# Two of four weight sums in a Strassen-Winograd product moved from VectorE to accumulating DMA

## The chip, the cores and the metric

The kernel runs on one core of one Trainium2 chip. A core has TensorE (matmuls), VectorE (DVE in the profile), ScalarE (ACT), GpSimd (POOL) and SyncE (SP), which work side by side and meet at semaphores, and 16 DMA engines that move data between DRAM and SBUF. The metric is the time of one launch on the device, in microseconds (us); lower is better.

## The reference

One block of a transformer-like network on 512 tokens with 2048 features, all in float32. What matters here is its last part, the feed-forward network:

```python
def conv_ffn(h, w_up, conv_w, conv_b, w_down):
    u, g = jnp.split(h @ w_up, 2, -1)
    return (u * jax.nn.silu(dwconv3(g, conv_w, conv_b))) @ w_down
...
        hx = modulate(x, sh2, sc2)
        fx = from_rows(conv_ffn(to_rows(hx), w_up[l], ffn_conv_w[l], ffn_conv_b[l], w_down[l]))
        x = layer_norm(ALPHA * x + g2 * fx, ln2_g[l], ln2_b[l])
```

`w_up` is 2048 x 11264 (two halves of 5632 columns, `u` and `g`) and `w_down` is 5632 x 2048. The depthwise convolution runs over rows of 64 tokens. Ahead of it stand a modulation from `w_ada`, an input projection, a gated recurrence in two directions, pooling and convolution mixers, and an output projection.

## The kernel before

The kernel runs through stages in this order: input projection and modulation (`ramp`), the recurrence and the other mixers (`heads`, `local`), the output projection (`out_half`), the up product (`up_half` for the first two pairs of column blocks, `up_pair` for the other 20) and the down product (`down`, `finish`). A scheduler sets the order of each engine's instructions from the order of the code and from priorities; loads and splits of weights stand under `high_priority(offset=AHEAD)`, so they come in the queues some 600 instructions earlier than the code has them. Tiles come from pools with a number of buffers per tag; a load waits until the buffer's last reader is done.

Matmuls reach float32 precision by splitting each operand into a high part H (a cast to `float32r` on ScalarE) and a low part L (the difference, on VectorE), with three matmuls for a product (`mm3`, lines 109 to 111: high by high, low by high, high by low).

The up product of a pair of column blocks (256 columns) is done by Winograd's form of Strassen's scheme: the 2048 x 256 weights are cut into halves by rows and by columns, the tokens into two halves of 256, and seven products of half size take the place of eight. The scheme needs four sums of the activations (`S1` to `S4`, made once in `combine`), four sums of the weights (made for each block in `weights7`), and sums of the products (`Z`, at the end of `up_block`). A tile `W` has, for each of its row blocks of 128, seven slots of 128 columns: four raw quarters and the four sums, one of which is built in place of a raw quarter. In numbers: slots 0 and 1 are the lower rows' left and right columns, slot 2 is the upper left, and slot 3 holds the upper right until the first sum is written over it.

`up_pair` runs `up_block` for the `g` half of the columns, the gate (`gate_conv`, the sigmoid and a product), `up_block` for the `u` half, and the last product with its store to DRAM (`h_d`). `up_block` has eight row blocks. Before, `weights7` loads and sums four of them at once (`NB`), in a tile with two buffers: two loads of 512 KB on SyncE's queue, three VectorE operations (lines 971 to 973, of which the first makes two sums), and then, for each two row blocks (`NU`, a unit), `parts`: one cast on ScalarE (line 954) and one difference on VectorE (line 955), into tiles H and L with three buffers each. TensorE runs the 42 matmuls of a unit product by product, in the order `for pr in (1, 2, 3, 7, 5, 6, 4)`. There are 20 pairs, 2 blocks each, 4 units a block: 160 units.

`down` takes the weights of the down product in loads of up to six row blocks of 512 columns, in the same `W` tag, and splits three at a time. `finish` does the last three row blocks together with the closing layer norm.

Of the kernel before, what the change touches and what calls it, by code (L numbers as in the profile page):

```python
# [40 lines left out]
NB, NU = 4, 2  # L41
# [31 lines left out]
class Kernel:  # L73
# [810 lines left out]
    def combine(self, cp, raw, k2s):  # L884
# [37 lines left out]
    def up_half(self, cp, p, hf):  # L922
# [15 lines left out]
        for i in range(2):  # L938
# [3 lines left out]
            s = cp.tile([P, n], F32, name=f"cs_{f}_{hf}", tag="cs", bufs=2)  # L942
# [15 lines left out]
    def weights7(self, ww, name, src, c0):  # L958

        nc = self.nc
        tt = nc.vector.tensor_tensor
        with self.tc.high_priority(offset=AHEAD):
            W = ww.tile([P, NB, 7, P], F32, name=f"W_{name}", tag="W", bufs=2)
            for r0, s0 in ((c0, 2), (c0 + KT // 2, 0)):
                nc.sync.dma_start(out=vw(W[:, 0, 0, :], [[7 * P, NB], [1, 2 * P]], s0 * P),
                                  in_=src[r0 * P:(r0 + NB) * P].rearrange("(k p) c -> p k c", p=P))
            pair = lambda a, b: vw(W[:, 0, 0, :], [[7 * P, NB], [(b - a) * P, 2], [1, P]], a * P)  # L970
            tt(out=pair(4, 3), in0=pair(3, 1), in1=pair(2, 3), op=ALU.subtract)  # L971
            tt(out=W[:, :, 5], in0=W[:, :, 1], in1=W[:, :, 4], op=ALU.subtract)
            tt(out=W[:, :, 6], in0=W[:, :, 0], in1=W[:, :, 5], op=ALU.subtract)  # L973
            units = []
            for c in range(0, NB, NU):
                units += self.parts(ww, f"{name}_{c}", W[:, c:c + NU].rearrange("p a s m -> p (a s m)"), 7 * NU * P),
        return units

    def up_block(self, ww, ep, name, src):
# [19 lines left out]
        tt = nc.vector.tensor_tensor
        Z = ep.tile([P, 6, 256], F32, name=f"Z_{name}", tag="Z", bufs=2)  # L1000
# [6 lines left out]
        tt(out=two(2, 3), in0=vw(X[2][:, :], [[0, 2], [1, 256]]), in1=two(4, 5), op=ALU.add)  # L1007
# [58 lines left out]
    def weights_down(self, ww, name, pieces):  # L1066

        nc = self.nc
        with self.tc.high_priority(offset=AHEAD):
            n = sum(m for _, m in pieces)  # L1070
            W = ww.tile([P, 7, 512], F32, name=f"W_{name}", tag="W", bufs=2)
            o = 0
            for src, m in pieces:
                nc.sync.dma_start(out=W[:, o:o + m], in_=src.rearrange("(k p) c -> p k c", p=P))
                o += m
            out = []
            for a in range(0, n, 3):
                m = min(3, n - a)
                H, Lw = self.parts(ww, f"{name}_{a}", W[:, a:a + m].rearrange("p k c -> p (k c)"), 512 * m)
                out += [(H[:, 512 * i:512 * i + 512], Lw[:, 512 * i:512 * i + 512]) for i in range(m)]  # L1080
        return out

    def down(self, ww, dn, f0, n, first):
        w = self.I["w_down"][0]
# [4 lines left out]
        for j in range(4):  # L1089
            banks = self.banks4(f"dn_{f0}_{j}")  # L1090
            for q0 in range(0, n, 6):
                m = min(6, n - q0)
                r0 = (f0 + q0) * P
                wt = self.weights_down(ww, f"dn_{f0}_{j}_{q0}", [(w[r0:r0 + m * P, 512 * j:512 * j + 512], m)])
# [9 lines left out]
    def finish(self, ww, cp, f0, n):  # L1104
        nc, I, w = self.nc, self.I, self.I["w_down"][0]
        for f in range(f0, f0 + n):
            self.load_h(cp, f)
        cols = lambda j: (w[f0 * P:(f0 + n) * P, 512 * j:512 * j + 512], n)
        wt = self.weights_down(ww, "rs_0", [cols(0), cols(1)])
        with self.tc.high_priority(offset=AHEAD):  # L1110
            W = ww.tile([P, 7, 512], F32, name="W_rs_1", tag="W", bufs=2)
            R = ww.tile([P, 7, 512], F32R, name="R_rs_1", tag="W", bufs=2)
            for i, j in enumerate((3, 2)):
                nc.sync.dma_start(out=W[:, i * n:(i + 1) * n], in_=cols(j)[0].rearrange("(k p) c -> p k c", p=P))
# [119 lines left out]
```

## Time and profile before

| | |
|---|---|
| median of three runs | 2746.2 us (2740.33 to 2747.18) |
| the profiled execution: time, span | 2748.07 us, 2746.3 us |
| mean granted TensorE clock | 0.981 |
| moved by DMA | 416.14 MB, mean 152 GB/s |
| GpSimd instructions in the stage from 1425 to 2245 us | none |

A row of the stage view gives the busy time of each engine in one stretch of the span. A row of the wait view reads: engine and line that waited, what it waited for, total us, number of times, the longest. A row of the group view gives line, engine, operation, output and inputs with their shapes, count, busy us and mean ns, then the idle time of the engine just before. A row of the tile view gives the shortest, median and longest duration in ns and the first and the last start. A row on DMA issues ends with the size of one transfer and the median time from issue to landing. A row of the timeline gives start, duration, engine, line and, in brackets, the idle time before it and what ended it.

### The profile page before, as it was taken

How to read it: one execution, taken by the hardware profiler on the slowest of the kernel's cores; microseconds unless marked ns; L12 is line 12 of the kernel's file. 1: busy time of each engine (PE TensorE's matmuls, PEld its weight loads, DVE VectorE, ACT ScalarE, POOL GpSimd, SP SyncE). 2: the span in 40 equal slices, each digit the busy share in tenths (PEclk: the TensorE clock that was granted, in tenths of full speed). 3: DMA queues.
4: the chain of work that ended last, by engine and by line, in shares of the span. 5: the costliest groups of instructions: out<-in, count | busy, mean ns of one | idle time of the engine just before them, and what ended most of it. 6: DMA issues, size and time to landing. Idle time of an engine off the chain costs nothing.

```text
span 2746.3 us, 39980 instructions
## 1 busy us (share of the span) xinstructions
PE 2579.1 (94%) x16332; PEld 2257.9 (82%) x16332; DVE 1891.1 (69%) x2390; ACT 939.5 (34%) x1127; POOL 219.9 (8%) x207
## 2 busy tenths in 40 slices
PE   5999999989898999989879999999999999999996
PEld 4677978778787787768879999999999988888885
DVE  5543777585867856677888878988889875334338
ACT  4222532232323223344544433433434433222111
POOL 0111022040403100000100000000000000000004
PEclk8999999999999999999989999999999999999998
DMA  8755444636364566675633333333333365433321
GB/s 270 245 195 172 123 150 148 203 104 200 112 196 130 165 200 197 211 237 176 198 122 112 113 108 113 111 123 113 111 110 121 116 207 184 142 134 98 136 92 62
DMA packets 311124, 416.14 MB, mean 152 GB/s; under 512 B 17860, under 2 KB 200476, under 8 KB 310428
## 3 DMA queue, kind: packets, MB, share of 16 engines
q1 hardware_dynamic: 310940, 413.59, 47.1%
q8 instruction: 128, 2.10, 0.4%
q14 instruction: 56, 0.46, 0.1%
HBM read 393.59 MB, written 19.93 MB: 151 GB/s over the span
## 4 chain that ended last, share of the span: by engine, by line
PE 37%; DMA 26%; DVE 25%; issue 6%; ACT 2%; POOL 2%; SPq 1%; DVEq 0%; ACTq 0%; POOLq 0%
DMA a<-in_w_ada_dram 11%; DMA W_u<-in_w_up_dram 6%; PE dn L109 5%; PE dn L110 5%; PE dn L111 5%; DMA W_g<-in_w_up_dram 5%; DVE L_g L955 3%; DVE aacc L674 3%; DVE L_u L955 3%; DVE W_u L971 2%; DVE W_g L971 2%; PE rc L109 1%; PE rc L111 1%; PE wo L110 1%; PE rc L110 1%
## 5 line engine op out<-in xcount | busy, mean ns | idle before, releaser
L674 DVE SCALAR_TENSOR_TENSOR aacc<-a,csil,aacc 128x512 f32<-128x512 f32 x240 | 185.0, 771 | 162.5 <-DMA a<-in_w_ada_dram 160.7
L955 DVE TENSOR_TENSOR L_dn<-W_dn,H_dn 128x1536 fp32r<-128x1536 f32 (+1 forms) x56 | 96.2, 1718 | 204.3 <-ACT H_dn L954 204.3
L954 ACT CAST H_u<-W_u 128x1792 fp32r<-128x1792 f32 x80 | 133.6, 1691 | 252.1 <-DVE W_u L973 194.4
L109 PE MATMUL dn<-H_dn,hh 128*128 128x512 f32 x480 | 186.6, 390 | 2.7 <-ACT hh L1052 2.7
L955 DVE TENSOR_TENSOR L_u<-W_u,H_u 128x1792 fp32r<-128x1792 f32 x80 | 161.6, 2019 | 37.8 <-ACT H_u L954 37.7
L110 PE MATMUL dn<-L_dn,hh 128*128 128x512 f32 x480 | 186.9, 389 | 0.0
L111 PE MATMUL dn<-H_dn,hl 128*128 128x512 f32 x480 | 186.7, 390 | 0.0
L954 ACT CAST H_dn<-W_dn 128x1536 fp32r<-128x1536 f32 (+1 forms) x56 | 81.2, 1451 | 272.7 <-PE dn L111 272.6
L954 ACT CAST H_g<-W_g 128x1792 fp32r<-128x1792 f32 x80 | 135.0, 1694 | 115.0 <-DVE W_g L973 64.3
L955 DVE TENSOR_TENSOR L_g<-W_g,H_g 128x1792 fp32r<-128x1792 f32 x80 | 161.4, 2018 | 3.3 <-ACT H_g L954 3.2
L109 PE MATMUL ub_g<-h2h,H_g 128*128 128x256 f32 x480 | 134.4, 280 | 16.0 <-ACT H_g L954 16.0
L111 PE MATMUL ub_u<-h2h,L_u 128*128 128x256 f32 x480 | 136.7, 285 | 12.5 <-DVE L_u L955 11.7
L111 PE MATMUL ub_g<-h2h,L_g 128*128 128x256 f32 x480 | 135.2, 282 | 12.2 <-DVE L_g L955 12.1
L123 POOL TENSOR_TENSOR ln_r<-ln_e,mhalf 128x1 f32<-128x1 f32 x12 | 9.3, 785 | 1657.0 <-DVE ln_e L118 1421.8
L109 PE MATMUL ub_u<-h2h,H_u 128*128 128x256 f32 x480 | 134.5, 280 | 0.0
L110 PE MATMUL ub_u<-h2l,H_u 128*128 128x256 f32 x480 | 134.1, 279 | 0.0
L110 PE MATMUL ub_g<-h2l,H_g 128*128 128x256 f32 x480 | 133.9, 279 | 0.0
L104 DVE TENSOR_TENSOR wl_wo<-wr_wo,wh_wo 128x1024 fp32r<-128x1024 f32 x64 | 78.3, 1223 | 49.0 <-ACT wh_wo L103 48.9
L109 PEld LDWEIGHTS dn<-H_dn,hh 128*128 128x128 f32 x480 | 90.1, 188 | 22.6 <-ACT hh L1052 4.0
L110 PE MATMUL wo<-wl_wo,oh 128*128 128x512 f32 x256 | 102.6, 401 | 4.9 <-DVE wl_wo L104 4.8
L111 PEld LDWEIGHTS dn<-H_dn,hl 128*128 128x128 f32 x480 | 90.1, 188 | 19.8 <-DVE hl L1053 1.1
L110 PEld LDWEIGHTS dn<-L_dn,hh 128*128 128x128 f32 x480 | 90.1, 188 | 18.9 <-DVE L_dn L955 0.4
(445 smaller groups left out, 8377.0 us busy)
## 6 DMA issues: line engine op xcount, KB each, us to landing
a<-in_w_ada_dram SPq DMA_DIRECT2D x256, 256.0 KB, 3.3
W_g<-in_w_up_dram SPq DMA_DIRECT2D x80, 512.0 KB, 4.6
W_u<-in_w_up_dram SPq DMA_DIRECT2D x80, 512.0 KB, 4.7
W_dn<-in_w_down_dram SPq DMA_DIRECT2D x24, 1536.0 KB, 6.8
wr_wo<-in_w_out_dram SPq DMA_DIRECT2D x64, 512.0 KB, 4.1
ada<-in_w_ada_dram SPq DMA_DIRECT2D x56, 512.0 KB, 5.2
wr_r<-in_w_in_dram SPq DMA_DIRECT2D x48, 512.0 KB, 3.7
wr_up<-in_w_up_dram SPq DMA_DIRECT2D x32, 512.0 KB, 4.5
```

The costliest lines, as they stand in the source:

```text
L104: (lo_engine or nc.vector).tensor_tensor(out=lo, in0=raw, in1=hi.bitcast(F32), op=ALU.subtract)
L109: mm(out=out, lhsT=st[0], rhs=mv[0], start=start, stop=False)
L110: mm(out=out, lhsT=st[0], rhs=mv[1], start=False, stop=False)
L111: mm(out=out, lhsT=st[1], rhs=mv[0], start=False, stop=stop)
L123: nc.gpsimd.tensor_tensor(out=r, in0=t, in1=self.mhalf[:, 0:n], op=ALU.pow)
L674: nc.vector.scalar_tensor_tensor(out=acc, in0=raw, scalar=self.csil[:, k:k + 1], in1=acc, op0=ALU.mult, op1=ALU.add)
L954: nc.scalar.copy(out=H[:, 0:n], in_=src)
L955: nc.vector.tensor_tensor(out=Lw[:, 0:n], in0=src, in1=H[:, 0:n].bitcast(F32), op=ALU.subtract)
L971: tt(out=pair(4, 3), in0=pair(3, 1), in1=pair(2, 3), op=ALU.subtract)
```

## The change

The weight sums take a form with other signs in which all four are plain additions: slot 3 = upper left + upper right, slot 4 = upper right + lower right, slot 5 = slot 1 + slot 3, slot 6 = slot 0 + slot 5. Slots 3 and 4 are no longer made on VectorE. SyncE's queue loads the upper rows' two quarters into slots 3 and 4, the lower rows' into slots 0 and 1, and the upper left once more into slot 2; then two DMAs on GpSimd's queue read the upper right and the lower right from DRAM and add them onto slots 3 and 4. VectorE adds slots 5 and 6. The signs are carried into `combine` and into the sums of products, where one operation in each becomes `scalar_tensor_tensor`. A `W` tile now holds one unit of two row blocks, with four buffers in place of two of double size, so `down` and `finish` load three row blocks at a time. Products 5 and 7 change places in the order. `Z` and the `cs` tile of `up_half` have one buffer in place of two, and `dynamic_dma_scratch_size` is 1024 in place of 256.

```diff
-NB, NU = 4, 2
+NU = 2
...
+            stt = nc.vector.scalar_tensor_tensor
             tt(out=a11, in0=a11, in1=a21, op=ALU.subtract)
-            tt(out=a21, in0=a21, in1=a22, op=ALU.add)
-            tt(out=a22, in0=a22, in1=a11, op=ALU.subtract)
-            tt(out=a12, in0=a12, in1=a22, op=ALU.subtract)
+            tt(out=a21, in0=a22, in1=a21, op=ALU.subtract)
+            stt(out=a22, in0=a22, scalar=-1.0, in1=a11, op0=ALU.mult, op1=ALU.subtract)
+            tt(out=a12, in0=a12, in1=a22, op=ALU.add)
...
-            s = cp.tile([P, n], F32, name=f"cs_{f}_{hf}", tag="cs", bufs=2)
+            s = cp.tile([P, n], F32, name=f"cs_{f}_{hf}", tag="cs", bufs=1)
...
         with self.tc.high_priority(offset=AHEAD):
-            W = ww.tile([P, NB, 7, P], F32, name=f"W_{name}", tag="W", bufs=2)
-            for r0, s0 in ((c0, 2), (c0 + KT // 2, 0)):
-                nc.sync.dma_start(out=vw(W[:, 0, 0, :], [[7 * P, NB], [1, 2 * P]], s0 * P),
-                                  in_=src[r0 * P:(r0 + NB) * P].rearrange("(k p) c -> p k c", p=P))
-            pair = lambda a, b: vw(W[:, 0, 0, :], [[7 * P, NB], [(b - a) * P, 2], [1, P]], a * P)
-            tt(out=pair(4, 3), in0=pair(3, 1), in1=pair(2, 3), op=ALU.subtract)
-            tt(out=W[:, :, 5], in0=W[:, :, 1], in1=W[:, :, 4], op=ALU.subtract)
-            tt(out=W[:, :, 6], in0=W[:, :, 0], in1=W[:, :, 5], op=ALU.subtract)
-            units = []
-            for c in range(0, NB, NU):
-                units += self.parts(ww, f"{name}_{c}", W[:, c:c + NU].rearrange("p a s m -> p (a s m)"), 7 * NU * P),
-        return units
+            W = ww.tile([P, NU, 7, P], F32, name=f"W_{name}", tag="W", bufs=4)
+            slots = lambda i, n: W[:, :, i:i + n].rearrange("p k s c -> p k (s c)")
+            nc.sync.dma_start(out=slots(3, 2), in_=rows(0, slice(0, 2 * P)))
+            nc.sync.dma_start(out=slots(0, 2), in_=rows(1, slice(0, 2 * P)))
+            nc.sync.dma_start(out=slots(2, 1), in_=rows(0, slice(0, P)))
+            for half in range(2):
+                nc.gpsimd.dma_start(out=W[:, :, 3 + half], in_=rows(half, slice(P, 2 * P)), accum_op=ALU.add)
+            tt(out=W[:, :, 5], in0=W[:, :, 1], in1=W[:, :, 3], op=ALU.add)
+            tt(out=W[:, :, 6], in0=W[:, :, 0], in1=W[:, :, 5], op=ALU.add)
+            return self.parts(ww, name, W.rearrange("p a s m -> p (a s m)"), 7 * NU * P)
...
-                for pr in (1, 2, 3, 7, 5, 6, 4):
+            for pr in (1, 2, 3, 5, 7, 6, 4):
...
-        Z = ep.tile([P, 6, 256], F32, name=f"Z_{name}", tag="Z", bufs=2)
+        Z = ep.tile([P, 6, 256], F32, name=f"Z_{name}", tag="Z", bufs=1)
...
-        tt(out=two(2, 3), in0=vw(X[2][:, :], [[0, 2], [1, 256]]), in1=two(4, 5), op=ALU.add)
+        nc.vector.scalar_tensor_tensor(out=two(2, 3), in0=two(4, 5), scalar=-1.0,
+                                       in1=vw(X[2][:, :], [[0, 2], [1, 256]]), op0=ALU.mult, op1=ALU.subtract)
...
+        W = ww.tile([P, 7 * NU * P], F32, name=f"W_{name}", tag="W", bufs=4)
+        nc.sync.dma_start(out=W[:, 0:512 * m].rearrange("p (k c) -> p k c", c=512),
+                          in_=self.I["w_down"][0][r0:r0 + m * P, 512 * j:512 * j + 512].rearrange("(k p) c -> p k c", p=P))
...
-    nc = bacc.Bacc("TRN2", target_bir_lowering=False, num_devices=1, dynamic_dma_scratch_size=256)
+    nc = bacc.Bacc("TRN2", target_bir_lowering=False, num_devices=1, dynamic_dma_scratch_size=1024)
```

SyncE's queue at pair 10 of the up product, before. In a name such as `W_g10_0` stand the half of the columns, the pair and the part of the block; the last number counts tiles; `h_d18` is a store of pair 9's result:

```order
L968 DMA W_g10_0_15474<-in_w_up_dram 128x4x256 x2
L968 DMA W_g10_1_15572<-in_w_up_dram 128x4x256 x2
L968 DMA W_u10_0_15695<-in_w_up_dram 128x4x256 x2
L1027 DMA h_d18_98<-cv_18_15245 128x512
L1027 DMA h_d19_99<-cv_19_15252 128x512
L968 DMA W_u10_1_15793<-in_w_up_dram 128x4x256 x2
```

The same queue from the `u` half of pair 10 on, after:

```order
L971 DMA W_u10_0_16035<-in_w_up_dram 128x2x256
L972 DMA W_u10_0_16035<-in_w_up_dram 128x2x256
L973 DMA W_u10_0_16035<-in_w_up_dram 128x2x128
L971 DMA W_u10_2_16089<-in_w_up_dram 128x2x256
L972 DMA W_u10_2_16089<-in_w_up_dram 128x2x256
L973 DMA W_u10_2_16089<-in_w_up_dram 128x2x128
L971 DMA W_u10_4_16143<-in_w_up_dram 128x2x256
L972 DMA W_u10_4_16143<-in_w_up_dram 128x2x256
L973 DMA W_u10_4_16143<-in_w_up_dram 128x2x128
L1029 DMA h_d18_98<-cv_18_15545 128x512
L1029 DMA h_d19_99<-cv_19_15552 128x512
L971 DMA W_u10_6_16197<-in_w_up_dram 128x2x256
```

Three loads stand for each two row blocks where two stood for four, and the two stores come after three of the block's four units instead of after half of the block.

GpSimd's queue has nothing between the last product of `up_half` (line 945) and the closing layer norm before; after, it has two accumulating transfers for each unit, one right after the other:

```order
L975 DMA W_g10_0_15794<-in_w_up_dram 128x2x128 x2
L975 DMA W_g10_2_15848<-in_w_up_dram 128x2x128 x2
L975 DMA W_g10_4_15902<-in_w_up_dram 128x2x128 x2
L975 DMA W_g10_6_15956<-in_w_up_dram 128x2x128 x2
L975 DMA W_u10_0_16035<-in_w_up_dram 128x2x128 x2
```

These rows run on without a break over all 160 units, 320 transfers.

VectorE at the same place, before (Z is the sums of the products of the block that ends, cv the gate of the pair before):

```order
L971 TENSOR_TENSOR W_g10_0_15474<-W_g10_0_15474 128x4x2x128
L917 SCALAR_TENSOR_TENSOR cv_18_15245<-Z_g9_15238,col_c_656,cv_18_15245 128x8x63
L972 TENSOR_TENSOR W_g10_0_15474<-W_g10_0_15474 128x4x128
L919 SCALAR_TENSOR_TENSOR cv_18_15245<-Z_g9_15238,col_d_662,cv_18_15245 128x8x63
L955 TENSOR_TENSOR L_u9_1_2_15372<-W_u9_1_15361,H_u9_1_2_15371 128x1792
L973 TENSOR_TENSOR W_g10_0_15474<-W_g10_0_15474 128x4x128
```

and after:

```order
L976 TENSOR_TENSOR W_g10_0_15794<-W_g10_0_15794 128x2x128
L977 TENSOR_TENSOR W_g10_0_15794<-W_g10_0_15794 128x2x128
L1006 TENSOR_TENSOR Z_g9_15538<-ub_g9_1_15319,P1_g9_15539 128x2x256
L1007 TENSOR_TENSOR Z_g9_15538<-ub_g9_0_15318,Z_g9_15538 128x256
L1008 SCALAR_TENSOR_TENSOR Z_g9_15538<-Z_g9_15538,ub_g9_2_15320 128x512
L1010 TENSOR_TENSOR Z_g9_15538<-ub_g9_3_15321,Z_g9_15538 128x2x256
L956 TENSOR_TENSOR L_u9_4_15680<-W_u9_4_15671,H_u9_4_15679 128x1792
L976 TENSOR_TENSOR W_g10_2_15848<-W_g10_2_15848 128x2x128
L918 SCALAR_TENSOR_TENSOR cv_18_15545<-Z_g9_15538,col_c_656,cv_18_15545 128x8x63
```

The three operations on four row blocks are now two short ones on each two, and one of them stands between two low halves (L).

More of the change, by code (lines that the diff above doesn't have):

```diff
@@ L964, in weights7 @@
         tt = nc.vector.tensor_tensor
+        r = src.shape[0] // 2
+        rows = lambda half, cols: src[half * r + c0 * P:half * r + (c0 + NU) * P, cols].rearrange("(k p) c -> p k c", p=P)
         with self.tc.high_priority(offset=AHEAD):
[L966 to L977 removed]
+            W = ww.tile([P, NU, 7, P], F32, name=f"W_{name}", tag="W", bufs=4)
[8 more added lines that the diff above has]
+            return self.parts(ww, name, W.rearrange("p a s m -> p (a s m)"), 7 * NU * P)
     def up_block(self, ww, ep, name, src):
@@ L1064, in acc_y, with raw_down, weights_down @@
             nc.vector.tensor_tensor(out=yc, in0=yc, in1=tmp, op=ALU.add)
-    def weights_down(self, ww, name, pieces):
+    def raw_down(self, ww, name, r0, m, j):
         nc = self.nc
-        with self.tc.high_priority(offset=AHEAD):
[L1070 to L1081, printed above, removed]
+        W = ww.tile([P, 7 * NU * P], F32, name=f"W_{name}", tag="W", bufs=4)
+        nc.sync.dma_start(out=W[:, 0:512 * m].rearrange("p (k c) -> p k c", c=512),
+                          in_=self.I["w_down"][0][r0:r0 + m * P, 512 * j:512 * j + 512].rearrange("(k p) c -> p k c", p=P))
+        return W[:, 0:512 * m]
+    def weights_down(self, ww, name, r0, m, j):
+        with self.tc.high_priority(offset=AHEAD):
+            H, Lw = self.parts(ww, name, self.raw_down(ww, name, r0, m, j), 512 * m)
+        return [(H[:, 512 * i:512 * i + 512], Lw[:, 512 * i:512 * i + 512]) for i in range(m)]
     def down(self, ww, dn, f0, n, first):
-        w = self.I["w_down"][0]
         for f in range(f0, f0 + n):
@@ L1090, in down @@
             banks = self.banks4(f"dn_{f0}_{j}")
[L1091 to L1094, printed above, removed]
+            for q0 in range(0, n, 3):
+                m = min(3, n - q0)
+                wt = self.weights_down(ww, f"dn_{f0}_{j}_{q0}", (f0 + q0) * P, m, j)
                 for jj in range(m):
@@ L1104, in finish @@
     def finish(self, ww, cp, f0, n):
-        nc, I, w = self.nc, self.I, self.I["w_down"][0]
+        nc, I = self.nc, self.I
         for f in range(f0, f0 + n):
             self.load_h(cp, f)
[L1108 to L1114, printed above, removed]
-            nc.scalar.copy(out=R[:, 0:n], in_=W[:, 0:n])
-            nc.vector.tensor_tensor(out=R[:, n:2 * n], in0=W[:, 0:n], in1=R[:, 0:n].bitcast(F32), op=ALU.subtract)
-            H, Lw = self.parts(ww, "rs_2", W[:, n:2 * n].rearrange("p k c -> p (k c)"), 512 * n)
-        res = {(f0 + i, j): wt[j * n + i] for i in range(n) for j in range(2)}
-        for i in range(n):
-            res[f0 + i, 2] = (H[:, 512 * i:512 * i + 512], Lw[:, 512 * i:512 * i + 512])
-            res[f0 + i, 3] = (R[:, i], R[:, n + i])
+        res = {}
+        for j in (0, 1, 3, 2):
+            if j == 3:
+                with self.tc.high_priority(offset=AHEAD):
+                    raw = self.raw_down(ww, "rs_3", f0 * P, n, j)
+                    H, Lw = (ww.tile([P, 7 * NU * P], F32R, name=f"W{nm}_rs_3", tag="W", bufs=4) for nm in "hl")
+                    nc.scalar.copy(out=H[:, 0:512 * n], in_=raw)
+                    nc.vector.tensor_tensor(out=Lw[:, 0:512 * n], in0=raw, in1=H[:, 0:512 * n].bitcast(F32), op=ALU.subtract)
+                wt = [(H[:, 512 * i:512 * i + 512], Lw[:, 512 * i:512 * i + 512]) for i in range(n)]
+            else:
+                wt = self.weights_down(ww, f"rs_{j}", f0 * P, n, j)
+            for i in range(n):
+                res[f0 + i, j] = wt[i]
         rows = {}
```

24 lines of the change are left out of this document (12 added, 12 removed).

## The prediction

> **What bounds the kernel now.** I read the page's first two parts, then the busy times by stage, then TensorE's waits in the stage that the change rewrites, then that stage's transfers.
>
> ```profile
> PE 2579.1 (94%) x16332; PEld 2257.9 (82%) x16332; DVE 1891.1 (69%) x2390; ACT 939.5 (34%) x1127; POOL 219.9 (8%) x207
> ...
> PE   5999999989898999989879999999999999999996
> ...
> DVE  5543777585867856677888878988889875334338
> ...
> POOL 0111022040403100000100000000000000000004
> ```
> Slices 21 to 32 are the block-product stage (`up_block`): TensorE at 9, VectorE at 8 or 9, GpSimd at 0.
>
> ```profile
> 1425.00:2245.00 820.00, 795.27 (x6617) 787.35 (x6616) 700.83 (x714) 329.67 (x283) 0.00 (x0) 0.99 0.36 117
> 2245.00:2640.00 395.00, 392.26 (x1720) 321.87 (x1719) 157.89 (x168) 93.58 (x88) 0.00 (x0) 1.00 0.43 144
> ...
> PE ub_g L111 <- DVE L_g L955: 12.1, 9, 2.5
> PE ub_u L111 <- DVE L_u L955: 11.7, 9, 3.0
> ```
> The columns of the first two rows are stretch, length, then PE, PEld, DVE, ACT and POOL busy, granted clock, DMA share, GB/s. TensorE is busy 795.3 of 820 us, so 24.7 us is idle; the two wait rows (12.1 + 11.7 = 23.8 us) say that it waits for the low halves that VectorE makes. VectorE is busy 700.8 us, 85%. In the down stage behind it only 2.7 us is idle. So TensorE bounds the stage, and a lighter VectorE can give back at most about 25 us.
>
> The stage's two ends:
> ```profile
> 1393.69 2.04 SPq L968 DMA_DIRECT2D W_g<-in_w_up_dram  x4
> ...
> 1404.93 0.58 PE L109 MATMUL ub_g<-h2h,H_g 128*128 128x256 f32 x1 [15.99 <-ACT H_g L954]
> ...
> 2236.22 0.39 PE L109 MATMUL dn<-H_dn,hh 128*128 128x512 f32 x1
> ```
> The first weights are asked for at 1393.7, the first product runs at 1404.9, and the down stage's first matmul at 2236.2. The products take 831.3 us for 160 units of two row blocks (20 pairs, 2 blocks each, 4 units a block): **5.20 us a unit**.
>
> **The change part by part.** *VectorE, removed and added.*
> ```profile
> L955 DVE TENSOR_TENSOR L_g<-W_g,H_g x80: 2010/2018/2026, 1404.9 to 2209.3; 128x1792 fp32r<-128x1792 f32 x80
> L971 DVE TENSOR_TENSOR W_g<-W_g x40: 1224/1226/1228, 1400.3 to 2196.4; 128x1024 f32<-128x1024 f32 x40
> L972 DVE TENSOR_TENSOR W_g<-W_g x40: 683/689/695, 1401.5 to 2197.6; 128x512 f32<-128x512 f32 x40
> L973 DVE TENSOR_TENSOR W_g<-W_g x40: 681/691/694, 1402.3 to 2198.4; 128x512 f32<-128x512 f32 x40
> ...
> L1007 DVE TENSOR_TENSOR Z_g<-ub_g,Z_g 128x512 f32<-128x512 f32 x20 | 13.8, 691 | 0.7
> L1006 DVE TENSOR_TENSOR Z_g<-ub_g,Z_g 128x256 f32<-128x256 f32 x20 | 8.5, 424 | 0.7
> ...
> L919 DVE SCALAR_TENSOR_TENSOR cv<-Z_g,col_d,cv 128x504 f32<-128x504 f32 x40 | 29.6, 740 | 0.7
> ```
> Per group of four row blocks the adds cost 1.226 + 0.689 + 0.691 = 2.61 us; 80 groups (40 for `g`, as many for `u`) make 208.5 us. After, 160 units have two adds of 128x256 each; the nearest row is L1006, 0.424 us, so 320 x 0.424 = 135.7 us. One of the four closing operations of each block becomes SCALAR_TENSOR_TENSOR: 40 x (0.740 - 0.691) = 2.0 us more. VectorE sheds about 71 us, from 85% of the stage to 77%. It is not on TensorE's path except for the 23.8 us of waits.
>
> *TensorE and ScalarE.* Products 5 and 7 change places, the number of matmuls and casts is the same: nothing. `combine` keeps its number of operations.
>
> *SyncE's queue.* Three loads a unit (256 + 256 + 128 KB) in place of two of 512 KB for two units: 480 issues, not 160.
> ```profile
> L968 SPq DMA_DIRECT2D W_g<-in_w_up_dram x80: 367/502/520, 1393.7 to 2189.7; - x80
> ```
> At 0.50 us each a unit holds SyncE 1.5 us of 5.20. The `h_d` stores stand behind three of the next `u` block's four units where they stood behind half of it; loads and stores are issued well ahead of their use, so I cost them at nothing. The cover is the four W buffers, which hold one block as before; if a load comes late, the cast of H behind it is late next.
>
> *GpSimd's queue, the disputed term.* 320 accumulating transfers, two a unit, each 128 KB from DRAM added onto 128 KB in SBUF. They stand between the plain loads and the unit's adds and cast: a link that was not there. GpSimd does nothing else in this stage (0.00 us), so nothing else is queued behind its wait; what waits is the first add on VectorE (whose queue also holds the older units' low halves and the gates) and the cast on ScalarE, which reads the whole tile, and then TensorE. The profile has no accumulating transfer and none from this queue. Nearest rows, issue to landing:
> ```profile
> h_d<-cv SPq DMA_DIRECT2D x36, 256.0 KB, 2.0
> ...
> a<-in_w_ada_dram SPq DMA_DIRECT2D x256, 256.0 KB, 3.3
> W_g<-in_w_up_dram SPq DMA_DIRECT2D x80, 512.0 KB, 4.6
> W_u<-in_w_up_dram SPq DMA_DIRECT2D x80, 512.0 KB, 4.7
> ...
> q1 hardware_dynamic: 82000, 85.72, 34.4%
> ```
> Low bound 2.0 us (the stores), high bound 4.7 us (512 KB loads). An accumulation reads 256 KB and writes 128 KB; the 256 KB loads read and write 256 KB each and come from DRAM as it does, so I take their **3.3 us**. Whether two accumulations are under way at once decides. One queue issues them, the unit's second directly behind its first, and the room for their lists is 1024 bytes a partition (`dynamic_dma_scratch_size`). I take it that the second goes only when the first is done. Then a unit costs GpSimd's queue 2 x 3.3 = 6.6 us against TensorE's 5.20, and the queue sets the stage.
>
> Sum: first landing 1393.7 + 4.6 = 1398.3; 320 x 3.3 = 1056 us brings the last accumulation to 2454.3; behind it the cast of 1.7 (row L954 of the page, 1694 ns) and one unit of products, 5.2, to 2461.2, against 2236.2 before: **+225 us**.
> ```profile
> L954 ACT CAST H_g<-W_g 128x1792 fp32r<-128x1792 f32 x80 | 135.0, 1694 | 115.0 <-DVE W_g L973 64.3
> ```
> What speaks against this: the Trainium skill, "DMA: Bandwidth & Descriptors", section "Anatomy of one DMA", puts a transfer from GpSimd at 2.0 us plus its bytes over 436 GB/s. For 128 KB that is an estimate of 2.3 us, 320 of them 736 us, less than the 831 of the products, and the accumulations would be hidden (the first rival's time). For 256 KB it gives 2.6 us, where the row above has 3.3 us; no run here shows a transfer from GpSimd. On the other side, the Trainium skill, the same page, "Terms" and "SWDGE vs HWDGE vs iDMA" says that such a transfer's descriptors, 16 bytes each, stand in rings in a carved-out piece of SBUF; the Trainium skill, "Collectives: The Full Stack", section "The bandwidth ceiling", says that an add takes two reads for one write. By an estimate from these, 256 rows over 16 engines are 32 reads and an end mark, and 64 places do not hold two such lists. No row here shows a ring.
>
> *Sizes elsewhere.* `Z` with one buffer: a block's result is used up within the first part of the next block, 20 us before the next is written; nothing. `cs` with one buffer in `up_half`: the second half's sigmoid waits for the first's product, and the last store precedes the W loads on SyncE's queue.
> ```profile
> 1384.92 1.76 POOL L945 TENSOR_TENSOR cs<-cv,cs 128x256 f32<-128x256 f32 x1 [1.13 <-ACT cs L944]
> ...
> 1392.87 0.68 DVE L900 TENSOR_TENSOR S4l<-a,S4h 128x512 fp32r<-128x512 f32 x1
> ```
> The cover is VectorE's combining, which ends at 1393.55. Bounds 0 and about 2.5 us once (one more GpSimd product, 1.76, and VectorE's product behind it); I take 1. `down` and `finish`: 768 KB loads, four buffers, the same bytes; with 2.7 us idle in 395 the stage has next to nothing to gain. I take nothing; bounds -3 (the idle time) and +3 (as much again).
>
> Total +226 on the profiled execution's 2748.1 us, 2974.1; the median of the three runs is 1.9 lower, so **2972 us**.
>
> **The rivals.** *1. The accumulations are hidden, and the kernel is faster.* Either two run at once or one takes under 831.3 / 320 = 2.60 us; that is the point from which it decides. For it: the stores' 2.0 us, and DMA at 36% of the stage. Against it: no load of 256 KB shows under 3 us in the median. Then TensorE's 24.7 us of idle time shrink, since VectorE has 71 us more and makes a unit's adds in 0.85 us at a stretch, where now a chain of 2.6 us for four blocks holds up the low halves. Two thirds of it back, less 1: 2746 - 15 = **2731 us**, between 2721 and 2738.
>
> *2. Hidden, but nothing comes of it.* The link of 3 to 7 us lengthens the way from buffer to buffer, and the waits for L stay: 2746 within 8 us. For it: VectorE itself waits for loads in this stage, so a freer VectorE may only wait longer.
> ```profile
> DVE W_u L971 <- DMA W_u<-in_w_up_dram: 40.6, 38, 3.4
> ...
> DVE W_g L971 <- DMA W_g<-in_w_up_dram: 31.4, 27, 3.7
> ```
> These 72 us are as much as it would shed. Within 0.3% (8 us) is what a measurement of this kernel cannot tell from no change.
>
> *3. The DMA engines become the bound.* From q1's row, 82000 packets took 34.4% of 760 us of 16 engines (the stretch 1440 to 2200): 51 ns each, mostly of 1 KB. A unit now has 512 such packets; after, 512 of 1 KB, 256 of 512 bytes, and 512 accumulated rows with two reads each, 1024. If the half-size ones cost as much as full ones, 1792 x 51 / 16 = 5.7 us a unit, 160 units 914 us, +83: **2829 us**. If cost goes by bytes, 640 KB + 2 x 256 KB against 512 KB is 34.4% x 2.25 = 77%, and this is hidden. It speaks for a slower kernel even where accumulations overlap.
>
> **How the numbers follow.** One at a time above 2.6 us: 0.55, as the 256 KB loads stand on that side and their issue is by hardware, which this one's is not known to be; its own range is 2812 to 3196 us (2.8 to 4.0 us each). DMA engines: 0.10. Hidden and faster: 0.24. Hidden and the same: 0.11. So slower 0.65, same 0.11, faster 0.24. The range, 2726 to 3190, leaves out some 0.03 of the faster case and 0.12 with accumulations of 4 us and more.
>
> **What would show it.** Right: in the stage TensorE waits for casts and low halves that wait for `W` transfers of GpSimd's queue, a unit every 6 to 7 us, the stage 200 to 250 us longer, accumulations never overlapping, VectorE's adds at 0.42 us. Rival 1: TensorE above 98% in the stage, GpSimd's queue with free time between accumulations. Rival 3: DMA share near 0.9 there. The prediction fails if an accumulation takes under 2.6 us or two overlap; it comes out too low if GpSimd needs over a microsecond of its own before each, or if TensorE's clock falls in the gaps.

## The result and the profile after

The changed kernel takes **3323.6 us** (median of four runs, 3317.99 to 3325.83), the kernel before 2746.7 us on the same chip: a ratio of 1.2108, interval 1.2084 to 1.2132. The direction was forecast; the time (2972 us, at most 3190) was not.

The page's engines and slices, after:

```profile
PE 2759.2 (83%) x16332; PEld 2420.5 (73%) x16332; DVE 1814.1 (55%) x2470; ACT 937.5 (28%) x1127; POOL 611.1 (18%) x527
...
PE   6999998999899999756667667777777768999997
...
POOL 0110122130400000122222222222222221000004
PEclk9999999999999999978888888788888888999998
```

TensorE stands at 5 to 8 in the block-product stage, where it stood at 9. In the stage view, the block-product stage and the down stage:

```profile
1425.00:2800.00 1375.00, 967.10 (x6616) 943.45 (x6615) 623.47 (x785) 325.94 (x277) 383.41 (x315) 0.84 0.52 114
2800.00:3210.00 410.00, 408.96 (x1832) 337.92 (x1832) 172.13 (x186) 102.37 (x99) 0.00 (x0) 1.00 0.43 146
```

TensorE is idle for 408 of 1375 us. From the first product at 1415.9 us to the down stage at 2808.6 us it is 1392.7 us, against 831.3 before: **8.70 us a unit** in place of 5.20. That is 561 of the 570 us by which the span grew (3316.2 against 2746.3). Another 11 us stand ahead of the stage's first product, and behind the stage it is 2.5 us shorter. The waits of the stage (1425 to 2790 us):

```profile
DVE W_u L976 <- DMA W_u<-in_w_up_dram: 381.3, 80, 7.5
DVE W_g L976 <- DMA W_g<-in_w_up_dram: 356.4, 78, 10.1
POOL W_u L975 <- issue: 345.1, 107, 5.1
POOL W_g L975 <- issue: 344.9, 99, 5.5
...
PE ub_g L111 <- DVE L_g L956: 204.3, 58, 6.5
```

TensorE waits for the low halves, VectorE for the accumulations, nearly once for each of the 160 units, and GpSimd for nothing that the profile can name ("issue"). What happens there stands in the timeline of GpSimd's queue and SyncE's:

```profile
1903.00 1.21 POOL L975 DMA_DIRECT2D W_g<-in_w_up_dram  x1 [2.59 <-issue]
1906.85 1.22 POOL L975 DMA_DIRECT2D W_g<-in_w_up_dram  x1 [2.64 <-DVE L_u L956]
1912.43 1.21 POOL L975 DMA_DIRECT2D W_g<-in_w_up_dram  x1 [4.35 <-issue]
1916.21 1.22 POOL L975 DMA_DIRECT2D W_g<-in_w_up_dram  x1 [2.56 <-DVE L_g L956]
...
1906.74 0.37 SPq L971 DMA_DIRECT2D W_g<-in_w_up_dram  x1
...
1916.17 0.37 SPq L971 DMA_DIRECT2D W_u<-in_w_up_dram  x1
```

Each accumulation holds GpSimd for 1.21 us, and the next never starts sooner than 2.46 us behind that: the shortest step from start to start is 3.68 us, the middle one 3.94. The one that starts at 1906.85, together with a later unit's loads, takes 5.6. "Issue" hides what GpSimd waits for, but the landings in the trace tell it: in all 319 steps the next accumulation starts 0.26 to 0.32 us behind the landing of the one before, so two are never under way at once. The page gives 3.6 us from issue to landing as the median; the mean is 4.03.

```profile
W_g<-in_w_up_dram POOLq DMA_DIRECT2D x160, 128.0 KB, 3.6
```

In the tile view the starts run over the whole stage:

```profile
L975 POOL DMA_DIRECT2D W_g<-in_w_up_dram x160: 1203/1213/1371, 1402.9 to 2756.5; - x160
L975 POOL DMA_DIRECT2D W_u<-in_w_up_dram x160: 1204/1213/1222, 1440.2 to 2789.9; - x160
```

From 1402.9 to 2789.9 there are 319 steps of **4.35 us**. Two make 8.70, the time of a unit. So the queue sets the stage, as forecast, with a price of 4.35 (4.03 to the landing and 0.32 to the next) where 3.3 was put.

### The profile page after: what moved, and what is told of

It reads as the page before. It is cut to its first block, busy times and chain, and to the rows that moved or that the text cites. A ratio compares the mean times of both kernels' runs of the same rounds, so it can differ in the third digit from the quotient of the medians.

```text
span 3316.2 us, 41978 instructions
## 1 busy us (share of the span) xinstructions
PE 2759.2 (83%) x16332; PEld 2420.5 (73%) x16332; DVE 1814.1 (55%) x2470; ACT 937.5 (28%) x1127; POOL 611.1 (18%) x527
## 3 DMA queue, kind: packets, MB, share of 16 engines
q0 software_dynamic: 87040, 41.96, 10.4%
## 4 chain that ended last, share of the span: by engine, by line
DMA 20%; DVE 16%; PE 15%; issue 6%; POOL 1%; SPq 0%; DVEq 0%; ACT 0%; ACTq 0%; POOLq 0%
DMA W_g<-in_w_up_dram 10%; DMA W_u<-in_w_up_dram 9%; DVE L_u L956 5%; PE dn L109 4%; PE dn L110 4%; PE dn L111 4%; DVE L_g L956 4%; DVE W_u L976 1%; DVE W_g L976 1%; PE ub_g L111 1%; DVE cv L920 1%; PE ub_g L109 1%; PE ub_g L110 1%; DMA hr<-h_d 1%; DVE Z_u L1008 0%
## 5 line engine op out<-in xcount | busy, mean ns | idle before, releaser
L111 PE MATMUL ub_g<-h2h,L_g 128*128 128x256 f32 x480 | 161.6, 337 | 206.4 <-DVE L_g L956 206.4
L111 PE MATMUL ub_u<-h2h,L_u 128*128 128x256 f32 x480 | 158.1, 329 | 192.9 <-DVE L_u L956 192.9
L975 POOL DMA_DIRECT2D W_g<-in_w_up_dram x160 | 194.9, 1218 | 511.5 <-issue 358.3
L975 POOL DMA_DIRECT2D W_u<-in_w_up_dram x160 | 194.7, 1217 | 493.3 <-issue 345.1
L111 PEld LDWEIGHTS ub_g<-h2h,L_g 128*128 128x128 f32 x480 | 109.0, 227 | 218.3 <-DVE L_g L956 218.3
L111 PEld LDWEIGHTS ub_u<-h2h,L_u 128*128 128x128 f32 x480 | 106.4, 222 | 204.7 <-DVE L_u L956 204.7
L976 DVE TENSOR_TENSOR W_u<-W_u 128x256 f32<-128x256 f32 x80 | 34.0, 425 | 381.3 <-DMA W_u<-in_w_up_dram 381.3
L976 DVE TENSOR_TENSOR W_g<-W_g 128x256 f32<-128x256 f32 x80 | 34.0, 425 | 373.8 <-DMA W_g<-in_w_up_dram 373.8
L109 PE MATMUL ub_g<-h2h,H_g 128*128 128x256 f32 x480 | 149.3, 311 | 29.1 <-ACT H_g L955 29.1
L110 PE MATMUL ub_g<-h2l,H_g 128*128 128x256 f32 x480 | 149.0, 310 | 0.0
```

What stands on the lines that cost most here:

```text
L109: mm(out=out, lhsT=st[0], rhs=mv[0], start=start, stop=False)
L110: mm(out=out, lhsT=st[0], rhs=mv[1], start=False, stop=False)
L111: mm(out=out, lhsT=st[1], rhs=mv[0], start=False, stop=stop)
L975: nc.gpsimd.dma_start(out=W[:, :, 3 + half], in_=rows(half, slice(P, 2 * P)), accum_op=ALU.add)
L976: tt(out=W[:, :, 5], in0=W[:, :, 1], in1=W[:, :, 3], op=ALU.add)
```

## The experiments

*Is it the room for the transfers' lists?* `e1_room` doubles it (and gives up a buffer of `yt` in the down stage to make place).

```diff
-    nc = bacc.Bacc("TRN2", target_bir_lowering=False, num_devices=1, dynamic_dma_scratch_size=1024)
+    nc = bacc.Bacc("TRN2", target_bir_lowering=False, num_devices=1, dynamic_dma_scratch_size=2048)
```

> The changed kernel with dynamic_dma_scratch_size 2048 instead of 1024, and one buffer instead of two for the scratch of the down stage's closing sums, to make the room. Theory S (GpSimd's queue works on one accumulation at a time because their lists have room for one, and at 4.3 us each 320 of them set the stage): with room for two or more they overlap, GpSimd's own 1.2 us for each is 2.4 us a unit against TensorE's 5.2, the stage is close to 831 us again, 2740 to 2830 us in all. Rival E (the DMA engines, with 2.25 times the bytes in smaller rows, are the bound): nothing changes, 3230 to 3400 us. Rival L (it is the length of the new link between the loads and the sums, with four buffers, that makes units late): unchanged to slightly shorter, 3100 to 3320 us.

Measured: 2967.5 us, ratio 1.0801 (1.078 to 1.0821): 356 us came back. Between the theories: the queue was the bound, and behind it stands another. The stage takes 6.50 us a unit. The turn that paces it, on VectorE, SyncE and GpSimd in the timeline of `e1_room`:

```profile
1919.29 2.02 DVE L956 TENSOR_TENSOR L_u<-W_u,H_u 128x1792 fp32r<-128x1792 f32 x1
...
1929.76 0.42 DVE L976 TENSOR_TENSOR W_g<-W_g 128x256 f32<-128x256 f32 x1 [3.94 <-DMA W_g<-in_w_up_dram]
...
1931.74 2.02 DVE L956 TENSOR_TENSOR L_g<-W_g,H_g 128x1792 fp32r<-128x1792 f32 x1
...
1921.33 0.37 SPq L971 DMA_DIRECT2D W_g<-in_w_up_dram  x1
...
1933.79 0.37 SPq L971 DMA_DIRECT2D W_u<-in_w_up_dram  x1
...
1924.91 2.44 POOL L975 DMA_DIRECT2D W_g<-in_w_up_dram  x2 [7.50 <-DMA W_g<-in_w_up_dram]
```

Two accumulations now go back to back (x2 in 2.44 us). But L ends at 1921.31 and frees a `W` buffer; a load starts at 1921.33; it lands and the accumulations start at 1924.91; the adds at 1929.76; behind them in VectorE's queue the next L, which ends at 1933.76; the next load but one starts at 1933.79. A turn of 12.5 us.

*The change without the accumulations.* `e2_dve` keeps all else (units of two, four buffers, the signs) and makes the sums on VectorE.

```diff
-            nc.sync.dma_start(out=slots(3, 2), in_=rows(0, slice(0, 2 * P)))
+            nc.sync.dma_start(out=slots(2, 2), in_=rows(0, slice(0, 2 * P)))
             nc.sync.dma_start(out=slots(0, 2), in_=rows(1, slice(0, 2 * P)))
-            nc.sync.dma_start(out=slots(2, 1), in_=rows(0, slice(0, P)))
-            for half in range(2):
-                nc.gpsimd.dma_start(out=W[:, :, 3 + half], in_=rows(half, slice(P, 2 * P)), accum_op=ALU.add)
+            pair = lambda a, b: vw(W[:, 0, 0, :], [[7 * P, NU], [(b - a) * P, 2], [1, P]], a * P)
+            tt(out=pair(4, 3), in0=vw(W[:, 0, 0, :], [[7 * P, NU], [0, 2], [1, P]], 3 * P), in1=pair(1, 2), op=ALU.add)
```

> The changed kernel without accumulations: two loads of 256 KB a unit, and the sums in slots 3 and 4 by one VectorE operation on 128 x 512. What is left is the form with other signs, units of two with four buffers, single buffers for Z and cs, loads of three in the down stage. All theories: the loss is in the accumulations, so 2735 to 2770 us; VectorE has 1.54 us of sums a unit against 1.30 before. If other parts of the change cost much, over 2800 us.

Measured: **2703.6 us**, ratio 0.9837 (0.9818 to 0.9856), the fastest of all. The stretch 1425 to 2200 us:

```profile
1425.00:2200.00 775.00, 775.00 (x6598) 774.18 (x6597) 706.83 (x938) 334.97 (x281) 0.00 (x0) 1.00 0.39 124
```

TensorE waits for nothing, with VectorE busy 91% of the time, more than before. So the accumulations cost the whole loss, and the waits for L that they were to remove go away without them. The stage takes 791.0 us, 40.3 less than before. Which of the parts that are left brings this was not taken apart.

*One accumulation, one sum on VectorE, in the changed kernel's own room:* `e3_one`.

```diff
-            for half in range(2):
-                nc.gpsimd.dma_start(out=W[:, :, 3 + half], in_=rows(half, slice(P, 2 * P)), accum_op=ALU.add)
+            nc.gpsimd.dma_start(out=W[:, :, 3], in_=rows(0, slice(P, 2 * P)), accum_op=ALU.add)
+            tt(out=W[:, :, 4], in0=W[:, :, 4], in1=W[:, :, 1], op=ALU.add)
```

> The changed kernel with one accumulation a unit (slot 3); slot 4 is added by VectorE. Theory S: 160 accumulations of 4 to 5 us need 640 to 800 us, less than the 831 of the products, so 2735 to 2770 us. Rival E: the accumulated rows are halved, so about half of the loss stays, 2950 to 3100 us. Rival L: the link of 4 to 5 us is there for each unit still, 3000 to 3200 us.

Measured: 2891.6 us, ratio 1.0524 (1.0495 to 1.0553). One accumulation a unit takes 3.9 us from issue to landing in the mean, of the 6.1 that the unit takes, so the queue is not the bound here. Three of four start later than 0.4 us behind the landing of the one before: GpSimd waits for the loads.

```profile
POOL W_u L974 <- DMA W_u<-in_w_up_dram: 202.0, 37, 7.3
...
DVE W_u L976 <- DMA W_u<-in_w_up_dram: 121.2, 60, 6.0
```

*The changed kernel's own room, lists half as long:* `e4_halves` cuts each accumulation into two of 64 KB.

```diff
-                nc.gpsimd.dma_start(out=W[:, :, 3 + half], in_=rows(half, slice(P, 2 * P)), accum_op=ALU.add)
+                for i in range(NU):
+                    r0 = half * r + (c0 + i) * P
+                    nc.gpsimd.dma_start(out=W[:, i, 3 + half], in_=src[r0:r0 + P, P:2 * P], accum_op=ALU.add)
```

> The changed kernel with each accumulation cut into two of one row block each (640 of 64 KB; the same bytes in the same rows). Theory S: lists of half the length leave room for three at a time in 1024 bytes; GpSimd's own 1.2 us for each is then 4.8 us a unit against 5.2, so 2745 to 2850 us. Rival E: the same bytes and rows, 3280 to 3400 us. Rival L: 3300 us or more.

Measured: 2978.1 us, ratio 1.0833 (1.0808 to 1.0857): with twice as many transfers nearly the same gain as from doubling the room. So the length of the list against the room decides, not the number of transfers.

From `e1`, `e3` and `e4` I formed theory C, the turn above. VectorE's queue is in order, and the adds of a unit stand ahead of the L of the unit two before it. Here is its order in `e1_room` (u9_4 and u9_6 are the third and fourth unit of a block, g10_0 and g10_2 the next two):

```
L956 TENSOR_TENSOR L_u9_4_15680<-W_u9_4_15671,H_u9_4_15679 128x1792
L976 TENSOR_TENSOR W_g10_2_15848<-W_g10_2_15848 128x2x128
L918 SCALAR_TENSOR_TENSOR cv_18_15545<-Z_g9_15538,col_c_656,cv_18_15545 128x8x63
L977 TENSOR_TENSOR W_g10_2_15848<-W_g10_2_15848 128x2x128
L920 SCALAR_TENSOR_TENSOR cv_18_15545<-Z_g9_15538,col_d_662,cv_18_15545 128x8x63
L956 TENSOR_TENSOR L_u9_6_15734<-W_u9_6_15725,H_u9_6_15733 128x1792
```

With four buffers the load of a unit waits for the L of the unit four before. So one turn through load, accumulation, adds and L passes only two units, not four. The kernel before has adds ahead of L too, but no accumulation in the turn.

*Take the turn apart.* `e5_room_order` is `e1_room` with the first add held behind that L, by a factor of one that is made from a column of it.

```diff
-            tt(out=W[:, :, 5], in0=W[:, :, 1], in1=W[:, :, 3], op=ALU.add)
+            past = self.__dict__.setdefault("past", [])
+            if len(past) >= 2:
+                one = ww.tile([P, 1], F32, name=f"one_{name}", tag="one", bufs=4)
+                nc.vector.tensor_scalar(out=one, in0=past[-2][:, 0:1].bitcast(F32), scalar1=0.0, scalar2=1.0, op0=ALU.mult, op1=ALU.add)
+                nc.vector.scalar_tensor_tensor(out=W[:, :, 5], in0=W[:, :, 1], scalar=one, in1=W[:, :, 3], op0=ALU.mult, op1=ALU.add)
...
+            past.append(HL[1])
```

> The kernel with room for three lists (2048), and VectorE's order changed: a unit's adds come directly behind the low half of the unit two before it, where they came directly ahead of it (the first add takes a factor of one that is made from that low half, so the order is forced). Theory C: with four W buffers and the adds of unit m ahead of L of unit m-2, one turn of load (about 4.0 us), accumulations (2.4 + 4.1), adds (0.85) and L (2.0), some 13 us, passes two units, 6.5 us each, as measured (1415 to 2455 for 160). Behind L of unit m-2 a turn passes three units, 4.4 us each, less than TensorE's 4.9, and the stage is bound by TensorE or by the DMA engines: 2700 to 2800 us. Rival E (DMA engines, 69% busy at 6.5 us a unit): 2900 to 2980 us. Rival L (the link is too long for four buffers, whatever the order): 2940 to 2980 us.

Measured: 2732.8 us, ratio 0.9956 (0.9936 to 0.9976); 235 us less than `e1_room`, by order alone.

```profile
1425.00:2200.00 775.00, 775.00 (x6556) 775.00 (x6555) 657.47 (x936) 333.81 (x278) 374.89 (x307) 1.00 0.93 200
```

TensorE has no gap, at a DMA share of 0.93. `e6_one_order` is `e3_one` with the same factor in both adds.

> The kernel with one accumulation a unit, with the same forced order, the VectorE add of slot 4 included. Theory C: a turn of load 4.0, accumulation 1.2 + 3.6, adds 0.9 and L 2.0, about 12 us, passes three units in place of two, 4.0 us each instead of 5.96, so TensorE bounds the stage as in the kernel without accumulations: 2695 to 2730 us. Rivals E and L: 2870 to 2900 us as without the order.

Measured: 2733.0 us, ratio 0.9961 (0.9943 to 0.9979), 3 us above the forecast; 159 us less than `e3_one`. The queue has next to no slack here either: every accumulation starts 0.26 to 0.32 us behind the landing of the one before, 4.94 us apart, beside 5.00 us of a unit's products. `e7_after_order` is the changed kernel, with its own room, and the same factor.

> The changed kernel with the same forced order and its scratch of 1024 as it is. Theory C with S: here GpSimd's queue, with one list at a time, is what bounds; 320 accumulations at 3.8 us alone and 5 to 6 us beside the loads need the same as before, so 3250 to 3330 us. If the order alone were the cause: 2900 us or less.

Measured: 3352.8 us, ratio 1.223 (1.2192 to 1.2268), 23 us above the forecast's end: where one accumulation goes at a time, the order of VectorE gains nothing. So there are two bounds, one behind the other. `e8_one_five` gives `e3_one` a fifth `W` buffer, in a pool of the up product's own.

> The kernel with one accumulation a unit and five W buffers instead of four in the up stage (which then has a pool of its own, so that the down stage's first weights are loaded only when it is over). The scheduler then puts the adds of unit m directly ahead of L of unit m-3. Theory C: the turn still passes two units, 5.96 us each: 2885 to 2925 us with the loss at the seam of the pools. Rival L (too few buffers): 2720 to 2800 us.

Measured: 2908.8 us, ratio 1.061 (1.0578 to 1.0642), as expected: the scheduler puts the adds one unit further ahead, and a turn still passes two units. More buffers do not take the place of order.

*Why `e5` and `e6` are 29 us behind `e2`.* Their matmuls are slower by 1%, in the down stage too, where nothing of the change is at work. `e9_room_order_pad` is `e5` with a wider factor tile.

```diff
-                one = ww.tile([P, 1], F32, name=f"one_{name}", tag="one", bufs=4)
+                one = ww.tile([P, 16], F32, name=f"one_{name}", tag="one", bufs=4)[:, 0:1]
```

> Edit: the kernel with twice the room for GpSimd's transfers and with each unit's first add held behind the parts of the unit two before it, but with the four small tiles of the factor 64 bytes a partition wide instead of 4, so that every later tile stands at an address that is a multiple of 64 again. Theory A (the 1% by which all matmuls were slower there, 280 for 277 ns and 393 for 389, came from the tiles behind the small ones standing at odd addresses): matmuls at 276 and 389 ns, 2700 to 2712 us, level with the sums on VectorE (2703.6). Theory B (it came from the accumulations themselves or from the DMA engines at 93%): matmuls unchanged, 2728 to 2738 us.

Measured: 2720.5 us, ratio 0.9919 (0.9891 to 0.9947), between the two. In the tile views of `dn`, `e5_room_order`:

```profile
L109 PE MATMUL dn<-H_dn,hh x480: 390/393/501, 2205.4 to 2660.1; 128*128 128x512 f32 x160
```

and `e9_room_order_pad`:

```profile
L109 PE MATMUL dn<-H_dn,hh x480: 389/389/504, 2205.5 to 2649.5; 128*128 128x512 f32 x160
```

The matmuls are back at 389 ns, as theory A had it; in the block products the mean step from one matmul's start to the next, waits left out, falls from 118.3 to 117.1 ns, which is `e2`'s. The block-product stage takes 790.4 us, no more than `e2`'s 791.0. Of the 12.3 us between the two spans (2716.9 and 2704.6) 10.8 lie ahead of the first product, and of these 7.3 between the first weight load and it: 1400.1 to 1415.1 against 1396.6 to 1404.3. There the first accumulation is issued at 1403.8 and the first add runs at 1411.3, and no earlier unit's products cover that time. The other 3.5 are within what differs from run to run ahead of the stage: over the changed kernel and its variants the first weights are asked for between 1388.9 and 1402.6 us.

*What makes 4.35 us.* `e10_no_loads` leaves out two of each unit's three loads, and zeros stand in their place.

```diff
-            nc.sync.dma_start(out=slots(0, 2), in_=rows(1, slice(0, 2 * P)))
-            nc.sync.dma_start(out=slots(2, 1), in_=rows(0, slice(0, P)))
+            nc.vector.memset(slots(0, 3), 0.0)
```

> Edit: the changed kernel with the loads of slots 0 to 2 of each unit (384 of its 640 KB) left out and those slots set to zero by VectorE, so that their weights are left out of the product. What is left on SyncE's queue is one 256 KB load a unit. Theory P (the accumulation that runs beside the plain loads of a later unit is stretched from 3.8 to 5 or 6 us by them): most accumulations come at 3.8 us after one another, 320 of them in 1216 to 1290 us for 1389, in all 3130 to 3230 us. Theory Q (the longer ones are stretched by something else, such as GpSimd's own work on the gates or VectorE's order): as the changed kernel, 3300 to 3340 us.

Measured: 3259.6 us, ratio 1.188 (1.1825 to 1.1934), between the theories: 4.16 us a step. `e13_alone` leaves out the third as well (`memset(slots(0, 5), 0.0)`).

> Edit: the changed kernel with all three plain loads of each unit left out and slots 0 to 4 set to zero by VectorE, so that only the accumulations bring weights. Without two of the three loads the accumulations came every 4.16 us instead of 4.35. Theory P (what stretches some of them beyond 3.8 us are the plain loads): now 3.8 to 3.9 us after one another, 320 of them in 1216 to 1248 us, in all 3140 to 3180 us. Theory Q (something else, such as the stores of the gate's results or GpSimd's own work): 4.1 us or more, 3240 us or more.

Measured: 3234.6 us, ratio 1.1785 (1.1717 to 1.1852), again between the two, 5 us under the second's range, at 4.08 us a step. Counted in the timelines, from start to start: in the changed kernel 30% of the steps are over 4.5 us, with one load left 21%, with none 8%; the middle step goes from 3.94 to 3.92 to 3.87 us. In `e13_alone` 12 of the 27 long ones left stand behind VectorE, whose queue makes the zeros late:

```profile
POOL W_g L973 <- DVE cv L920: 39.0, 5, 8.0
...
POOL W_g L973 <- DVE W_g L971: 21.8, 4, 5.5
```

The landings separate the two. From issue to landing an accumulation takes 4.03 us in the mean in the changed kernel, 3.84 with one load left and 3.63 with none, and the next starts 0.32 us later; in `e13_alone` late zeros add 0.13. So alone a step takes 3.95 us, and the plain loads beside it make the other 0.40. The 3.95 are 1.2 of GpSimd's own work, 0.7 until the first packet moves, 1.4 of packets, 0.3 from the last packet to the landing and 0.3 to the next accumulation.

*Half lists and order, in the changed kernel's own room:* `e11_halves_order_pad` is `e4_halves` with `e9`'s factor (and with `yt`'s buffer given up to make place).

> Edit: the changed kernel with its own room, the accumulations cut into 640 of 64 KB, and each unit's first add held behind the parts of the unit two before it (small tiles 64 bytes wide). Theory: half lists overlap in that room, GpSimd's own work is 4 times 0.9, 3.6 us a unit below TensorE's 4.9, and no turn through VectorE's queue is left: 2695 to 2745 us. Rival (GpSimd at 3.6 of 4.9 us and two lists at a time are still too slow, the queue paces the stage): 2760 to 2990 us.

Measured: 2827.4 us, ratio 1.0303 (1.0265 to 1.0341): the rival. In its timeline three halves go back to back, and then GpSimd waits for room:

```profile
1903.55 2.69 POOL L977 DMA_DIRECT2D W_g<-in_w_up_dram  x3 [2.46 <-issue]
1907.59 2.70 POOL L977 DMA_DIRECT2D W_g<-in_w_up_dram  x3 [1.35 <-issue]
```

In `e9_room_order_pad`, with twice the room, three whole ones do the same:

```profile
1403.77 3.86 POOL L975 DMA_DIRECT2D W_g<-in_w_up_dram  x3 [6.18 <-DMA W_g<-in_w_up_dram]
1411.43 1.22 POOL L975 DMA_DIRECT2D W_g<-in_w_up_dram  x1 [3.80 <-issue]
```

One whole one in the single room, three halves there, three whole ones in the double room: the trace never shows more under way, and the next one starts no sooner than 0.25 us behind the landing of the oldest of them. The prediction's estimate from the Trainium skill, "DMA: Bandwidth & Descriptors", section "Terms" (descriptors of 16 bytes in rings in SBUF) gives, carried on, an estimated 33 places for a whole one and 17 for a half, in rooms of 64 and 128: 1, 3 and 3. The runs agree; they do not show the places themselves, and as by this count no run had room for a fourth, another limit of three at a time is not excluded.

*Is it the adding?* `e12_plain` is the changed kernel with the transfers as plain writes of the same bytes.

```diff
-                nc.gpsimd.dma_start(out=W[:, :, 3 + half], in_=rows(half, slice(P, 2 * P)), accum_op=ALU.add)
+                nc.gpsimd.dma_start(out=W[:, :, 3 + half], in_=rows(half, slice(P, 2 * P)))
```

> Edit: the changed kernel with the 320 transfers of GpSimd's queue as plain writes of the same bytes to the same places (nothing is added: slots 3 and 4 hold the second term alone, so two of the sums are left out). Theory G (the pace is that of GpSimd's queue in this room, whatever the transfer does at its end): as the changed kernel, 3290 to 3340 us. Theory H (the reading back and adding is what takes 2.6 us of the 3.8): a plain write lands sooner, the pace is under 3.5 us, 2750 to 3150 us.

Measured: 2866.0 us, ratio 1.0445 (1.0397 to 1.0494).

```profile
L975 POOL DMA_DIRECT2D W_g<-in_w_up_dram x160: 720/720/900, 1392.8 to 2309.3; - x160
...
1905.24 1.46 POOL L975 DMA_DIRECT2D W_g<-in_w_up_dram  x2 [5.69 <-DMA W_g<-in_w_up_dram]
```

A plain write costs GpSimd 0.72 us, not 1.21, two go back to back in the same room, and up to three are under way at once. GpSimd's queue moves 48 packets for each (15360 in all, most of 4096 bytes), where an accumulation has 272 (87040, most of 512 bytes). So it is the adding form of the transfer that is long for GpSimd and for the room. About 120 us above the kernel before are left. In the waits of 1440 to 2200 us there, GpSimd waits for the loads, not for "issue", and VectorE for the transfers, as in `e1_room`:

```profile
POOL W_g L975 <- DMA W_g<-in_w_up_dram: 187.9, 42, 9.1
...
DVE W_u L976 <- DMA W_u<-in_w_up_dram: 140.0, 43, 5.9
```

That speaks for the turn; plain writes with the forced order were not run.

## Why the prediction failed, point by point

- **The mechanism** was right: one accumulation at a time, since the room holds one list, and the queue sets the stage. In the trace each starts only when the one before has landed; `e1` gives more room, `e4` and `e12` need less of it, and in all three they overlap. Of the signs that it named, the adds at 0.42 us and the accumulations that never overlap came so; a unit every 6 to 7 us and a stage 200 to 250 us longer came as 8.70 and 561, by the next point.
- **The term of 3.3 us was mis-sized**, and it is the step that failed: 320 x 3.3 = 1056 us, where 319 steps took 1387. The row it came from times a plain load issued by SyncE, from issue to landing. The accumulation takes 3.63 us to its landing where no load runs beside it (`e13`), of which 1.21 are GpSimd's own work ahead of the transfer; the text had named that ("over a microsecond of its own before each") as what would make it too low, and priced it at nothing. The 0.32 us from a landing to the next start were put at nothing too. Plain loads beside it add 0.40 in the mean, and no row of before showed two queues side by side. The estimate from the Trainium skill, "DMA: Bandwidth & Descriptors", section "Anatomy of one DMA", 2.3 us, was further off; the measurement decides.
- **The range's own end, 4.0 us each**, was cut below its high bound of 4.7, which would have given 320 x 4.7 = 1504 us and held the result.
- **VectorE sheds 71 us**: 1891.1 to 1814.1, 77 us. Right, and worth nothing: `e2` has no wait of TensorE with VectorE at 91%.
- **"A lighter VectorE can give back at most about 25 us"** was wrong twice. `e2` gains 40.3 us in the stage, as the time behind a wait is slow too: busy time per matmul falls from 120.2 ns (795.27 us over 6617) to 117.5 (775.00 over 6598), which is some 18 us over 6720 matmuls. And it is not a lighter VectorE that gives it back, as `e2`'s is busier. The units of two with short adds between the low halves are the likely cause; `e2` does not part them from the other edits that it keeps.
- **Rival 1** needed two things at once, room and order. The text named the older units' low halves in VectorE's queue, and gave their place behind the adds no price; it is worth 235 us (`e1` to `e5`). With both, the time is 2720.5 (`e9`) or 2732.8 (`e5`), just under and inside the rival's 2721 to 2738. That is in part luck: the stage gives back about 41 us in `e9` where the rival had 16, and some 10 us are lost ahead of its first product where it had 1.
- **Rival 3** did not come: with no gap in TensorE the DMA share is 0.93 (`e5`). That is about 4.6 us a unit of 4.99 (797.7 us over 160), between its two costings (5.7 us by packets, 77% of the stage by bytes). Its two reads for each accumulated row do not show: an accumulation moves 256 packets of 512 bytes, of 66 ns each in the mean.
- **What was costed at nothing** stayed so: SyncE's queue (0.37 + 0.47 + 0.47 us a unit), the down stage (451.6 us from the first product's start to the last one's before, 449.3 after), and `Z`, which has its single buffer in `e2` too, where TensorE never waits. Of the 11 us ahead of the stage's first product, 5.5 lie behind the first weight load, where the new link stands, and 5.5 ahead of it; the 1 us for `cs` cannot be told apart from these.
- **The clock** fell in the gaps, to 0.84, but TensorE is not the bound there.

## What to carry to other kernels

Here an accumulating transfer from GpSimd's queue was priced by how many the queue could hold at once and by GpSimd's own work for it, and neither its bytes nor a load's landing time gave that price: work out how many go at once before anything else. When a new link comes between a load and the first instruction that uses it, look at what stands behind that instruction in its engine's order, and count how many units one turn through the buffers passes. And when a change has several parts, time it without its main one: here what was left without it was the gain.

## What the runs showed of the hardware

- GpSimd's own work for one transfer: 1.21 us for an accumulation of 256 rows of 512 bytes, 0.89 for 128 rows, 0.72 for a plain write of 256.
- Behind a long wait TensorE starts slowly. In the changed kernel a wait of 6.5 us is followed by some 5 us of matmuls that start every 0.21 us, then every 0.12; the granted clock there is 0.50 and then 1.00. Of the stage's 32 waits of 5 us and more, 31 are followed by such slow matmuls, of its 42 under 3 us only 3:

```profile
1900.49 0.58 PE L111 MATMUL ub_u<-h2h,L_u 128*128 128x256 f32 x1 [6.52 <-DVE L_u L956]
...
1905.14 0.41 PE L111 MATMUL ub_u<-S1h,L_u 128*128 128x256 f32 x1
...
1905.69 0.28 PE L111 MATMUL ub_u<-S3h,L_u 128*128 128x256 f32 x1
```

  The Trainium skill, "TensorE: Matmul & The Clock Gate", section "Part 1: The HAM clock gate", has it so: after at least one idle window of about 3.4 us the array gets half its clock, until a busy window has passed. By its 1.2 GHz 256 columns take an estimated 0.213 us; the trace agrees, with 0.21 us for 4.9 us.

- A tile of 4 bytes a partition made the matmuls behind it 1% slower (`e5` against `e9`: 393 and 389 ns in the down stage, 118.3 and 117.1 ns from start to start in the block products). That the tiles behind it then stand at odd addresses is the likely cause; only the width of the small tile was tried.
